# Two scan units of 64 groups in the S5 mixer, outputs multiplied from the states themselves, and another order of its steps

## The chip, the core and the metric

The kernel runs on one core of a Trainium2 chip. The metric is the device time of one execution in microseconds (us); less is better.

## The reference, cut to what matters

Two blocks in a row on 256 tokens of 1024 features. The first has a latent-attention layer and then an S5 layer, and a second block follows (two attentions and a gated feed-forward layer). The change lies in the S5 layer alone. It runs a diagonal complex state-space scan in two directions over 256 context tokens and then 256 latent tokens, for 128 groups of 16 channels with 64 complex states each:

```python
def step(h, u_chunk):
    bu = jnp.einsum('btgs,gps->btgp', u_chunk.astype(jnp.complex64), b_bar)
    a = jnp.broadcast_to(lam_bar, bu.shape)
    _, xs = lax.associative_scan(_ssm_combine, (a, bu), axis=1)
    xs = xs + powers[None] * h[:, None]
    y = jnp.einsum('btgp,gsp->btgs', xs, cmat).real
    return xs[:, -1], y
...
y = jax.nn.gelu(y.astype(g.dtype))
ya, yb = jnp.split(y @ w_glu + b_glu, 2, axis=-1)
return ((ya * jax.nn.sigmoid(yb)) * jax.nn.silu(g)) @ w_out
```

Here u and g are the two halves of `h @ w_in`, and y sums both directions and a skip term. Only the latent tokens are carried on.

## The kernel before, in words

Everything is float32; large products split an operand in a high and a low part and take three matmuls. Instructions are written in program order and a planner arranges them on each engine by its own costs, with the written order as priority, so that engines run in order but not always in the order of the text.

Tokens are held in chunks of 4, so that a direction has 64 chunks for the context and 64 for the latent tokens. The 128 partitions hold the 64 states of the forward direction (0 to 63) and of the backward one (64 to 127). The 128 groups are 16 tiles `m` of 8 groups. For each tile:

- `inputs(m)` multiplies `w_u` with the tokens, writes u to HBM (`ud`), and `take_back` reads it back in another layout (`U`).
- `chunk_sums(m)` multiplies U with the prepared input matrices `BT` (32 small matmuls), and ScalarE copies the results out: the context's sums to `Sc` (L1214), the latent ones to the unit's state array `Sl` (L1218). For every second tile a tree of VectorE operations (`scan_tree`, L1394) reduces the context to one state, which is put into `Cs` (L1226).
- `scan(un)` runs 63 sequential steps over the chunks of `Sl`, three VectorE operations each (`scan_step`, L1405: one multiplication to `ss`, two additions in place). `S5_UNITS` gives each of four units one block of 32 groups. `scan(...)` is a generator; `S5_PLAN` says how many steps of which units are written at which place, and two units named together are taken in turns.
- `direct(m)` starts the PSUM accumulation of the output with the part inside a chunk.
- `outputs(m)` (L1253) copies the states of the tile into `H` in chunk order, forward and backward (L1267 and L1268, ScalarE, the latter on VectorE for the tiles of `S5_DVE`), and multiplies `H` with `CC`: 16 matmuls with 128 rows. After each second tile ScalarE copies the sum to `Yb` (L1278), which goes to HBM (`yd`).
- `gate(m)` is the gate half of the projection with a Silu (L1285); `activate(b)` reads four tiles' y back, applies Gelu (L1294) and splits it; `glu(m)` begins the first six GLU tiles with the first half of y, and `s5_glu` (L1414) does the rest.

At the start of the kernel `s5_factors` (L920) makes the powers of the state matrix in `Lp` and the input factors in `Q` on VectorE; ScalarE copies them into the tables `FE` (L992 to L996).

Of the kernel before, what the change touches and what calls it, by code (L numbers as in the profile page):

```python
# [11 lines left out]
F32 = mybir.dt.float32  # L12
# [7 lines left out]
P = 128  # L20
# [62 lines left out]
S5_SPLIT = range(2, 8)  # L83
GLU_PLAIN = 3
GLU_EARLY = 6
S5_DVE = range(14, 16)
S5_UNITS = ((0,), (1,), (2,), (3,))

S5_PLAN = [("sums",0),("sums",1,(0,38)),("sums",2,(0,25),(1,25)),("sums",3,(1,25),(2,25)),("direct",0,4),("gates",0,5),("outputs",0,4),("scan",(1,13),(3,13)),("direct",4,8),("gates",5,13),("outputs",4,8),("direct",8,12),("scan",(2,38),(3,38)),("y",0,2),("gates",13,16),("outputs",8,12),("direct",12,16),("scan",(3,12)),("y",2,3),("glu",0,2),("outputs",12,16),("y",3,4),("glu",2,6)]

# [117 lines left out]
class Builder:  # L208
# [711 lines left out]
    def s5_factors(self, keep, pre):  # L920
# [37 lines left out]

        Lp = self.t(pre, [P, 2, P, 4]).rearrange("p r g s -> p r s g")
        ts(s2, cm, 1.0, None, ALU.add, ALU.bypass)  # L960
# [9 lines left out]

        Q = self.t(pre, [P, 2, P, 4]).rearrange("p r g s -> p r s g")
        self.tt(t1, re, re, ALU.mult)
# [166 lines left out]
    def s5(self):  # L1139
# [10 lines left out]
        ydw = self.yd.rearrange("(q j) o t c -> (j o t) q c", j=2)  # L1150
        U, Sl, Sc, Cs = {}, {}, {}, {}
        hh = []
# [35 lines left out]
        def chunk_sums(m):  # L1188
# [4 lines left out]
            if m == m0:  # L1193
                Sl[un] = [(late.pop(0) if late else self.s16([P, 4096])).rearrange("p (n r w) -> p n r w", r=2, w=w)
                          for _ in S5_UNITS[un]]
                Cs[un] = self.t(l1, [P, 2, w])
            if not od:
# [5 lines left out]
            for q in range(0, 4, 2):  # L1203
# [7 lines left out]
                for j in range(2):  # L1211
                    g0 = 2 * q + j
                    c0 = 8 * od + g0
                    nc.scalar.copy(S[:, :, :, c0:c0 + 3:2], ev(pS[j][:, :, :, 1]))  # L1214
                    c0 = 8 * (m - m0) + g0
                    for x, D in enumerate(Sl[un]):
                        n = D.shape[1]
                        nc.scalar.copy(D[:, :, :, c0:c0 + 3:2], ev(pS[j][:, :, :, 0, n * x:n * x + n]))  # L1218
            if not od:
# [3 lines left out]
            for l in range(6):  # L1223
                w, n = 1 << l, 32 >> l
                yield from self.scan_tree(S[:, w - 1::2 * w], S[:, 2 * w - 1::2 * w], LA[:, 4 * l:4 * l + 4], n)
            nc.vector.tensor_copy(Cs[un][:, :, 8 * (m - m0) - 8:8 * (m - m0) + 8], S[:, 63])  # L1226

        def scan(un):

            prev = Cs[un]  # L1230
            g0, w = 32 * S5_UNITS[un][0], 32 * len(S5_UNITS[un])
            n = 2048 // w
            for k in range(63):
                cur = Sl[un][k // n][:, k % n]
# [18 lines left out]
        def outputs(m):  # L1253
            un = unit[m // 4]
            C, S, m0 = Cs[un], Sl[un], 4 * S5_UNITS[un][0]
            CC = self.t(self.wp, [P, 8, 2, 64], F32, "wlo", 3)
            nc.sync.dma_start(out=CC.rearrange("p a b c -> p (a b c)"), in_=self.CCd[m])
            H = self.t(self.wp, [P, 2, 8, 64], F32, "whi", 3)
            g = slice(8 * (m - m0), 8 * (m - m0) + 8)
            hv = lambda x: x.rearrange("p c r g -> p r g c")  # L1260
            nc.scalar.copy(H[f, :, :, 0], C[f, :, g])
            nc.scalar.copy(H[b, :, :, 63], C[b, :, g])
            copy = nc.vector.tensor_copy if m in S5_DVE else nc.scalar.copy
            for x, D in enumerate(S):
                n = D.shape[1]
                k = min(n, 63 - n * x)
                nc.scalar.copy(H[f, :, :, 1 + n * x:1 + n * x + k], hv(D[f, :k, :, g]))  # L1267
                copy(H[b, :, :, 63 - n * x - k:63 - n * x], hv(D[b, k - 1::-1, :, g]))  # L1268
            py = pys.pop(m)
            for q in range(4):  # L1270
                for j in range(2):
                    for ri in range(2):
                        self.mm(py[64 * j:64 * j + 64, m % 2, q], CC[:, 2 * q + j, ri], H[:, ri, 2 * q + j], False,
                                m % 2 == 1 and q == 3 and ri == 1)
            done[m] = self.last
            if m % 2:
                Y = self.t(l1, [P, 8, 64], F32, "Yb", 2)
                nc.scalar.copy(Y, py.rearrange("p m q c -> p (m q) c"))  # L1278
                nc.scalar.dma_start(out=ydw[:, 4 * m - 4:4 * m + 4], in_=Y)

        def gate(m):
            ps = self.ps("b", (P, NL))
            self.linear32(ps, "w_u", 16 + m, self.h1, lat)
            sg = self.t(l1, [P, NL], F32, "sg", 2)
            nc.scalar.activation(sg, ps, AF.Silu)  # L1285
            nc.scalar.dma_start(out=self.sgd[m], in_=sg)

        def activate(b):
# [4 lines left out]
            nc.gpsimd.dma_start(out=y, in_=self.yd[32 * b:32 * b + 32].rearrange("(i g) o t c -> (g o) i (t c)", i=4))  # L1293
            nc.scalar.activation(y, y, AF.Gelu_apprx_tanh)  # L1294
            with self.tc.issue_after(self.step_last):
# [3 lines left out]
        def glu(m, k0=0, k1=KT, after=None):  # L1299

            if k0 == 0:
                self.pp.append(self.ps("a" if m < 4 else "b", (P, 2, NL)))
            pp = self.pp[m]
# [564 lines left out]
```

## Time and profile before

| what | us |
|---|---|
| median of 3 runs | 1421.99 |
| lowest, highest | 1419.64, 1423.6 |
| the profiled execution's own time | 1420.1 |
| its span, first to last instruction | 1418.3 |
| TensorE (PE) busy | 1343.9 (95%) |
| PE weight loads | 1146.2 (81%) |
| VectorE (DVE) busy | 1053.4 (74%) |
| ScalarE (ACT) busy | 826.2 (58%) |

The page is of one execution. Busy shares are averages over stages of different kinds; the S5 stage lies between about 500 and 810 us of the span.

### The profile page before, as it was taken

The page shows a single profiled execution, that of the slowest core. Times are in us where ns is not written, and L with a number is a line of the kernel's source. Part 1 is how long each engine was busy: PE and PEld are TensorE (multiplying, and loading weights), DVE is VectorE, ACT ScalarE, POOL GpSimd, SP SyncE. Part 2 cuts the span into 40 slices and gives each one's busy share as a digit, 9 for nine tenths or more (in the row PEclk, how much of TensorE's full clock was granted, in tenths as well). Part 3 has the DMA queues.
Part 4 walks back from the last instruction along what each step waited for, and adds up shares of the span by engine and source line. Part 5 has one row for each costly group of instructions (what it writes and reads, how often), then busy time and mean ns, then how long its engine had stood idle before and what let it go on. Part 6 is the DMA issues. An engine that isn't in the chain of part 4 may idle for free.

```text
span 1418.3 us, 26373 instructions
## 1 busy us (share of the span) xinstructions
PE 1343.9 (95%) x10042; PEld 1146.2 (81%) x10042; DVE 1053.4 (74%) x2546; ACT 826.2 (58%) x1433; POOL 95.7 (7%) x150
## 2 busy tenths in 40 slices
PE   5899999999999999788988999999999999999999
PEld 1577777887788667346877899999979999999999
DVE  6779768988789959899994465556667777788853
ACT  4598755665556854337367654444468664666642
POOL 1012100000012223220000000000000000000000
PEclk9999999999999999999999999999999999999999
DMA  8546633134275459665865766655434435555564
GB/s 307 203 172 225 200 116 127 56 116 139 85 269 188 145 163 317 211 195 145 249 211 190 247 206 197 191 188 186 155 110 133 143 130 164 173 185 180 185 185 136
DMA packets 105487, 252.60 MB, mean 178 GB/s; under 512 B 37168, under 2 KB 45744, under 8 KB 104976
## 3 DMA queue, kind: packets, MB, share of 16 engines
q1 hardware_dynamic: 77056, 204.50, 44.5%
q0 software_dynamic: 7344, 25.04, 5.4%
q10 hardware_dynamic: 20960, 21.37, 4.6%
q8 instruction: 79, 1.29, 0.4%
q14 instruction: 48, 0.39, 0.1%
HBM read 218.88 MB, written 34.08 MB: 178 GB/s over the span
## 4 chain that ended last, share of the span: by engine, by line
PE 70%; ACT 11%; DVE 8%; DMA 7%; issue 3%; ACTq 1%; POOL 0%; SPq 0%; POOLq 0%; DVEq 0%
PE a L228 57%; PE b L228 9%; DVE bt L284 2%; PE c L228 1%; ACT whi L240 1%; DMA ud<-Ub 1%; ACT whi L1267 1%; ACT zc L1102 1%; DVE wlo L284 1%; ACT whi L1268 1%; DMA raw<-in_w_glu 1%; ACT zc L1099 1%; DMA Ul<-Td 1%; PE c L671 1%; DVE s L284 1%
## 5 line engine op out<-in xcount | busy, mean ns | idle before, releaser
L228 PE MATMUL a<-s,whi 128*128 128x256 f32 (+2 forms) x3024 | 644.8, 310 | 2.1 <-ACT whi L240 2.1
L228 PEld LDWEIGHTS a<-s,whi 128*128 128x128 f32 x3024 | 494.0, 191 | 33.2 <-issue 4.3
L228 PE MATMUL a<-s,wlo 128*128 128x256 f32 (+1 forms) x1512 | 464.2, 309 | 0.6 <-DVE wlo L284 0.6
L284 DVE TENSOR_TENSOR wlo<-raw,whi 128x1024 fp32r<-128x1024 f32 (+2 forms) x234 | 280.8, 1201 | 193.7 <-ACT whi L240 192.7
L240 ACT CAST whi<-raw 128x1024 fp32r<-128x1024 f32 (+2 forms) x234 | 240.8, 1031 | 244.1 <-PE a L228 178.1
L228 PEld LDWEIGHTS a<-s,wlo 128*128 128x128 f32 x1512 | 289.3, 192 | 15.2 <-DVE wlo L284 1.2
L228 PE MATMUL a<-s,raw 128*128 128x512 f32 (+2 forms) x272 | 109.9, 556 | 17.7 <-DVE s L483 6.6
L228 PEld LDWEIGHTS a<-s,raw 128*128 128x128 f32 x272 | 53.8, 202 | 63.0 <-issue 38.6
L284 DVE TENSOR_TENSOR bt<-x,bc 128x512 f32<-128x512 f32 x128 | 83.4, 691 | 8.3 <-DMA bc<-in_bc 7.1
L284 DVE TENSOR_TENSOR s<-s,ss 128x64 f32<-128x64 f32 x504 | 87.6, 219 | 2.6
L228 PE MATMUL a<-x,whi 128*128 128x256 f32 (+1 forms) x384 | 74.2, 294 | 0.0
L284 DVE TENSOR_TENSOR ss<-x,s 128x128 f32<-128x128 f32 x248 | 62.5, 284 | 1.2
L228 PE MATMUL b<-s,raw 128*128 128x256 f32 x256 | 58.9, 387 | 3.1 <-ACT sg L1285 3.1
L228 PEld LDWEIGHTS a<-x,whi 128*128 128x128 f32 x384 | 60.4, 192 | 0.6
L228 PEld LDWEIGHTS b<-s,raw 128*128 128x128 f32 x256 | 48.4, 193 | 10.3 <-ACT sg L1285 3.7
L228 PE MATMUL a<-x,wlo 128*128 128x256 f32 (+1 forms) x192 | 56.1, 292 | 0.0
L284 DVE TENSOR_TENSOR sc<-LA,Sc 128x1024 f32<-128x1024 f32 (+5 forms) x96 | 44.2, 500 | 12.7 <-ACT Sc L1214 12.4
L228 PEld LDWEIGHTS a<-U,whi 64*64 64x64 f32 x1024 | 31.9, 140 | 21.3 <-ACT Ub L1178 10.7
L284 DVE TENSOR_TENSOR Sc<-Sc,sc 128x1024 f32<-128x1024 f32 (+5 forms) x96 | 48.0, 500 | 0.4
L228 PE MATMUL a<-U,whi 64*64 64x128 f32 x1024 | 37.5, 286 | 11.3 <-ACT Ub L1178 7.5
L733 DVE TENSOR_REDUCE st<-b 128x1 f32<-128x512 f32 (+1 forms) x64 | 34.8, 550 | 16.6 <-PE b L228 16.1
L240 ACT CAST s<-s 128x512 fp32r<-128x512 f32 (+1 forms) x48 | 25.9, 545 | 21.9 <-DVE s L284 14.8
(384 smaller groups left out, 2249.8 us busy)
## 6 DMA issues: line engine op xcount, KB each, us to landing
raw<-in_w_glu SPq DMA_DIRECT2D x64, 512.0 KB, 3.6
raw<-in_w_up SPq DMA_DIRECT2D x42, 512.0 KB, 3.5
raw<-in_w_out SPq DMA_DIRECT2D x40, 512.0 KB, 3.7
raw<-in_wmod SPq DMA_DIRECT2D x32, 512.0 KB, 3.6
raw<-in_w_u SPq DMA_DIRECT2D x32, 512.0 KB, 3.9
s<-in_wmod SPq DMA_DIRECT2D x16, 512.0 KB, 7.7
raw<-in_w_in SPq DMA_DIRECT2D x16, 512.0 KB, 4.3
BTd<-BT ACTq DMA_DIRECT2D x16, 512.0 KB, 3.5
```

Of the source, the lines that this page charges most:

```text
L228: self.last = self.ins(self.nc.tensor.matmul(out, l, r, start=start, stop=stop))
L240: self.nc.scalar.copy(hi, src)
L284: return self.ins(self.nc.vector.tensor_tensor(out, a, b, op=op))
L671: nc.tensor.transpose(pt[:, k, tt], pl[tt][:, (2 * b + k) * P:(2 * b + k + 1) * P], self.ident)
L733: nc.vector.tensor_reduce(st[:, 0:1], ps, axis=AX.X, op=ALU.max)
L1099: nc.scalar.copy(zt[b, :, 0:3], ct[b, :, 1:4])
L1102: nc.scalar.copy(zt[f, :, 4:7], ct[f, :, 0:3])
L1267: nc.scalar.copy(H[f, :, :, 1 + n * x:1 + n * x + k], hv(D[f, :k, :, g]))
L1268: copy(H[b, :, :, 63 - n * x - k:63 - n * x], hv(D[b, k - 1::-1, :, g]))
```

## The change

It gives each of two units two blocks (64 groups), so there are 126 steps of twice the width and no longer 252. The context's final state goes to slot 0 of `Sl`, the sums of chunk i to slot i + 1, so that the states stand where the outputs need them; `Cs` and `H` and their copies are gone, and `outputs` multiplies straight from `Sl`: for each group, part and state tile one matmul for the forward half (64 rows, into `py`) and one for the backward half read in reverse (64 rows, into a second PSUM tile `pb`), 32 columns each. `py` and `pb` are added on VectorE. Gelu is ordered behind the last gate's Silu. `Lp` and `Q` are laid out with the groups innermost. The GLU tiles 2 and 3 take PSUM tag "b", all others "a". `S5_PLAN` is another: sums 0 and 1 without scans, unit 0 scanned in sums 2 and 3 with five gates between them, unit 1 scanned alone in three parts after the sums.

```diff
-S5_DVE = range(14, 16)
-S5_UNITS = ((0,), (1,), (2,), (3,))
-S5_PLAN = [("sums",0),("sums",1,(0,38)),("sums",2,(0,25),(1,25)),("sums",3,(1,25),(2,25)),("direct",0,4),("gates",0,5),("outputs",0,4),("scan",(1,13),(3,13)),("direct",4,8),("gates",5,13),("outputs",4,8),("direct",8,12),("scan",(2,38),(3,38)),("y",0,2),("gates",13,16),("outputs",8,12),("direct",12,16),("scan",(3,12)),("y",2,3),("glu",0,2),("outputs",12,16),("y",3,4),("glu",2,6)]
+GLU_B = (2, 3)
+S5_UNITS = ((0, 1), (2, 3))
+S5_PLAN = [("sums",0),("sums",1),("sums",2,(0,30)),("gates",0,5),("sums",3,(0,33)),("direct",0,4),("gates",5,10),("outputs",0,4),("scan",(1,20)),("direct",4,8),("gates",10,14),("outputs",4,8),("scan",(1,20)),("direct",8,12),("gates",14,16),("y",0,2),("scan",(1,23)),("direct",12,16),("glu",0,2),("outputs",8,12),("y",2,3),("glu",2,4),("outputs",12,16),("y",3,4),("glu",4,6)]
...
-        Lp = self.t(pre, [P, 2, P, 4]).rearrange("p r g s -> p r s g")
+        Lp = self.t(pre, [P, 2, 4, P])
...
-        Q = self.t(pre, [P, 2, P, 4]).rearrange("p r g s -> p r s g")
+        Q = self.t(pre, [P, 2, 4, P])
...
                     for x, D in enumerate(Sl[un]):
                         n = D.shape[1]
-                        nc.scalar.copy(D[:, :, :, c0:c0 + 3:2], ev(pS[j][:, :, :, 0, n * x:n * x + n]))
+                        k = int(x == 0)
+                        nc.scalar.copy(D[:, k:, :, c0:c0 + 3:2], ev(pS[j][:, :, :, 0, n * x + k - 1:n * x + n - 1]))
...
-            H = self.t(self.wp, [P, 2, 8, 64], F32, "whi", 3)
...
-            for x, D in enumerate(S):
-                n = D.shape[1]
-                k = min(n, 63 - n * x)
-                nc.scalar.copy(H[f, :, :, 1 + n * x:1 + n * x + k], hv(D[f, :k, :, g]))
-                copy(H[b, :, :, 63 - n * x - k:63 - n * x], hv(D[b, k - 1::-1, :, g]))
-            py = pys.pop(m)
+            if m % 2 == 0:
+                pys["b"] = self.ps("a", (P, 2, 4, 64))
+            py, pb = pys.pop(m), pys["b"]
             for q in range(4):
-                for j in range(2):
-                    for ri in range(2):
-                        self.mm(py[64 * j:64 * j + 64, m % 2, q], CC[:, 2 * q + j, ri], H[:, ri, 2 * q + j], False,
-                                m % 2 == 1 and q == 3 and ri == 1)
+                for ri in range(2):
+                    for j in range(2):
+                        g = 2 * q + j
+                        for x, D in enumerate(S):
+                            n = D.shape[1]
+                            o = slice(64 * j, 64 * j + 64), m % 2, q
+                            end = m % 2 == 1 and q == 3 and ri == 1 and x == len(S) - 1
+                            v = D[:, :, ri, 8 * (m - m0) + g]
+                            self.mm(py[o][:, n * x:n * x + n], CC[f, g, ri], v[f], False, end)
+                            self.mm(pb[o][:, 64 - n * x - n:64 - n * x], CC[b, g, ri], v[b, ::-1],
+                                    m % 2 == 0 and q == 0 and ri == 0 and x == 0, end)
             done[m] = self.last
             if m % 2:
                 Y = self.t(l1, [P, 8, 64], F32, "Yb", 2)
-                nc.scalar.copy(Y, py.rearrange("p m q c -> p (m q) c"))
+                nc.scalar.copy(Y, pb.rearrange("p m q c -> p (m q) c"))
+                self.tt(Y, py.rearrange("p m q c -> p (m q) c"), Y, ALU.add)
...
-            nc.scalar.activation(sg, ps, AF.Silu)
+            self.gate_last = self.ins(nc.scalar.activation(sg, ps, AF.Silu))
...
-            nc.scalar.activation(y, y, AF.Gelu_apprx_tanh)
+            with self.tc.issue_after(self.gate_last):
+                nc.scalar.activation(y, y, AF.Gelu_apprx_tanh)
...
-                self.pp.append(self.ps("a" if m < 4 else "b", (P, 2, NL)))
+                self.pp.append(self.ps("b" if m in GLU_B else "a", (P, 2, NL)))
```

## Rows read from the trace of the kernel before

**Rows 1.** The page: its span, and the chain that ended last, by engine.

```profile
span 1418.3 us, 26373 instructions
...
PE 70%; ACT 11%; DVE 8%; DMA 7%; issue 3%; ACTq 1%; POOL 0%; SPq 0%; POOLq 0%; DVEq 0%
```

**Rows 2.** Windows: length, then busy of PE, PEld, DVE, ACT, POOL; clock; DMA.

```profile
560.00:600.00 40.00, 32.44 (x248) 16.35 (x247) 33.33 (x114) 13.99 (x37) 8.44 (x13) 0.91 0.73 231
700.00:800.00 100.00, 85.21 (x763) 75.39 (x762) 67.17 (x349) 71.76 (x80) 3.01 (x4) 0.97 0.69 214
560.00:800.00 240.00, 206.83 (x1830) 154.32 (x1829) 199.08 (x910) 133.77 (x218) 24.20 (x33) 0.95 0.67 206
```

**Rows 3.** Waits of PE, 560 to 800 us: total us, times, longest.

```profile
PE c L228 <- ACT whi L1268: 4.8, 3, 2.8
```

**Rows 4.** Timeline of DVE: the trees' copies to Cs of tiles 7 and 15, last scan step.

```profile
600.48 0.17 DVE L1226 COPY x<-Sc 128x32 f32<-128x32 f32 x1
...
685.73 0.17 DVE L1226 COPY x<-Sc 128x32 f32<-128x32 f32 x1
...
762.35 0.49 DVE L284 TENSOR_TENSOR s<-s,ss 128x64 f32<-128x64 f32 x2
```

**Rows 5.** Timeline of PE: runs of small matmuls, and one GLU tile's first half.

```profile
102.83 0.97 PE L228 MATMUL c<-zc,zb 128*32 128x112 f32 x32
...
565.95 1.98 PE L228 MATMUL a<-U,whi 64*64 64x128 f32 x64
...
684.56 2.55 PE L228 MATMUL c<-whi,wlo 128*64 128x64 f32 x78
...
749.65 7.17 PE L228 MATMUL a<-hl,raw 128*128 128x256 f32 x32 [2.72 <-DMA raw<-in_w_glu]
```

**Rows 6.** Groups by form, whole span: count, then busy us, mean ns, idle before.

```profile
L240 ACT CAST whi<-raw 128x1024 fp32r<-128x1024 f32 x220 | 230.4, 1049 | 230.4 <-PE a L228 168.6 <-issue 43.3 <-DMA raw<-in_w_up 4.2
...
L284 DVE TENSOR_TENSOR s<-s,ss 128x64 f32<-128x64 f32 x504 | 87.6, 219 | 2.6
...
L284 DVE TENSOR_TENSOR ss<-x,s 128x128 f32<-128x128 f32 x248 | 62.5, 284 | 1.2
...
L1267 ACT COPY whi<-s 64x1008 f32<-64x1008 f32 x16 | 31.4, 1960 | 2.1 <-DVE s L284 1.9
...
L1218 ACT COPY s<-a 128x256 f32<-128x256 f32 x64 | 27.2, 425 | 0.0
...
L228 PE MATMUL c<-whi,wlo 128*64 128x64 f32 x512 | 20.4, 233 | 4.8 <-ACT whi L1268 4.8
...
L284 DVE TENSOR_TENSOR sc<-LA,Sc 128x256 f32<-128x256 f32 x16 | 6.0, 417 | 0.1
...
L284 DVE TENSOR_TENSOR Sc<-Sc,sc 128x128 f32<-128x128 f32 x16 | 4.5, 282 | 0.1
```

**Rows 7.** Timeline of DVE: two neighbouring steps of interleaved scans, and of one alone.

```profile
744.29 0.49 DVE L284 TENSOR_TENSOR ss<-x,s 128x128 f32<-128x128 f32 x2
...
745.24 0.49 DVE L284 TENSOR_TENSOR ss<-x,s 128x128 f32<-128x128 f32 x2
...
760.33 0.29 DVE L284 TENSOR_TENSOR ss<-x,s 128x128 f32<-128x128 f32 x1
...
761.18 0.29 DVE L284 TENSOR_TENSOR ss<-x,s 128x128 f32<-128x128 f32 x1
```

**Rows 8.** Timeline of DVE and PE at the start: strided, unstrided, first large matmuls.

```profile
16.41 2.06 DVE L284 TENSOR_TENSOR cm<-x 128x512 f32<-128x512 f32 x2
...
28.38 2.49 DVE L284 TENSOR_TENSOR s<-s,s 128x512 fp32r<-128x512 f32 x4
...
26.58 6.26 PE L228 MATMUL a<-s,raw 128*128 128x512 f32 x8 [6.58 <-DVE s L483]
```

**Rows 9.** Timeline of ACT and PE: last copy of y, first of the second halves.

```profile
790.89 0.59 ACT L1278 COPY Yb<-c 128x512 f32<-128x512 f32 x1 [1.32 <-PE c L228]
...
808.86 0.40 PE L228 MATMUL a<-s,whi 128*128 128x256 f32 x2
```

More of the change, by code (lines that the diff above doesn't have):

```diff
@@ L1150, in s5 @@
         ydw = self.yd.rearrange("(q j) o t c -> (j o t) q c", j=2)
-        U, Sl, Sc, Cs = {}, {}, {}, {}
+        U, Sl, Sc = {}, {}, {}
         hh = []
@@ L1195, in chunk_sums @@
                           for _ in S5_UNITS[un]]
-                Cs[un] = self.t(l1, [P, 2, w])
             if not od:
@@ L1225, in chunk_sums @@
                 yield from self.scan_tree(S[:, w - 1::2 * w], S[:, 2 * w - 1::2 * w], LA[:, 4 * l:4 * l + 4], n)
-            nc.vector.tensor_copy(Cs[un][:, :, 8 * (m - m0) - 8:8 * (m - m0) + 8], S[:, 63])
+            nc.vector.tensor_copy(Sl[un][0][:, 0, :, 8 * (m - m0) - 8:8 * (m - m0) + 8], S[:, 63])
         def scan(un):
-            prev = Cs[un]
+            prev = Sl[un][0][:, 0]
             g0, w = 32 * S5_UNITS[un][0], 32 * len(S5_UNITS[un])
             n = 2048 // w
-            for k in range(63):
+            for k in range(1, 64):
                 cur = Sl[un][k // n][:, k % n]
@@ L1254, in outputs @@
             un = unit[m // 4]
-            C, S, m0 = Cs[un], Sl[un], 4 * S5_UNITS[un][0]
+            S, m0 = Sl[un], 4 * S5_UNITS[un][0]
             CC = self.t(self.wp, [P, 8, 2, 64], F32, "wlo", 3)
             nc.sync.dma_start(out=CC.rearrange("p a b c -> p (a b c)"), in_=self.CCd[m])
-            H = self.t(self.wp, [P, 2, 8, 64], F32, "whi", 3)
[L1259 to L1263, printed above, removed]
-            for x, D in enumerate(S):
-                n = D.shape[1]
-                k = min(n, 63 - n * x)
-                nc.scalar.copy(H[f, :, :, 1 + n * x:1 + n * x + k], hv(D[f, :k, :, g]))
-                copy(H[b, :, :, 63 - n * x - k:63 - n * x], hv(D[b, k - 1::-1, :, g]))
-            py = pys.pop(m)
-            for q in range(4):
-                for j in range(2):
-                    for ri in range(2):
-                        self.mm(py[64 * j:64 * j + 64, m % 2, q], CC[:, 2 * q + j, ri], H[:, ri, 2 * q + j], False,
-                                m % 2 == 1 and q == 3 and ri == 1)
+            if m % 2 == 0:
+                pys["b"] = self.ps("a", (P, 2, 4, 64))
+            py, pb = pys.pop(m), pys["b"]
+            for q in range(4):
+                for ri in range(2):
[9 more added lines that the diff above has]
+                                    m % 2 == 0 and q == 0 and ri == 0 and x == 0, end)
             done[m] = self.last
```

## The prediction, made before the changed kernel was run

> **What bounds the kernel now.** I read the page first: PE holds 70% of the chain that ended last, ACT 11%, DVE 8% [rows 1]. So time is won where PE idles and lost where PE gets more to do. The windows over the S5 stage show where it idles: from 560 to 800 us it is busy 206.8 of 240, which leaves 33.2 us, of them 7.6 before 600 (sums of tiles 4 to 7) and 14.8 after 700 [rows 2]; so 10.8 lie in 600 to 700. The waits say for what: one of the longer ones is the copies of the states, but it is only 4.8 us [rows 3]. The other engine to watch is DVE. Its last tree before 600 ends at 600.5, the last of all at 685.7, and the last scan step at 762.4 [rows 4]. From 600 to 700 it is the sums and scans that fill it; behind 762 PE works off what waited for the last states, and the first second half of the GLU begins at 808.9 [rows 9]. From there on the kernel is unchanged, so I ask by how much this 808.9 moves.
>
> **The change part by part.**
>
> *Outputs.* The copies go: 16 forward ones of 1.96 us, 31.4 us on ACT, and nearly as much for the backward ones [rows 6]. But ACT is not the bound; all PE ever waited for them is 4.8 us [rows 3], inside the 33.2. In return PE's work grows. Before, a tile has 16 matmuls; all 16 tiles together are 256, which the trace shows as 512 records, two for each float32 matmul, with 20.4 us busy [rows 6]. Now a tile has 4 x 2 x 2 groups and parts, two state tiles and two directions: 64 matmuls, 128 records; over 16 tiles 2048. Their price is the main unknown, since no row has 64 rows by 64 with 32 columns. The near ones are 0.97/32 = 30 ns (32 wide, 112 columns), 1.98/64 = 31 ns (64 by 64, 128 columns) and 2.55/78 = 33 ns (64 wide, 64 columns) [rows 5]. The columns differ by two and the price hardly, so I take 30.5 ns: 62.5 us, that is +42. The bounds: if the price fell with the columns, 31 x 32/128 = 8 ns, 16 us in all, -4. If the stream set the pace, see next, it is 62 ns and 127 us, +107.
>
> The states are read with a step of 128 floats, where H was unbroken. What a step costs is seen on other engines: ACT copies the stepped states at 1960/1008 = 1.94 ns per column and an unbroken tile at 1049/1024 = 1.02 [rows 6]; DVE takes 1.03 us for 512 strided columns against 0.62 for unbroken ones [rows 8]. On PE no row shows it. Thirty-two columns at 1.94 ns are 62 ns, the upper bound. I keep 30.5 because forward and backward halves sit on different partitions, so that two streams at 62 would still give 31 per record.
> The Trainium skill ("SBUF — State Buffer", section "Door 1: The DMA port swizzle") says that SBUF has 16-byte lines and that each access to a new line pays; the ACT and DVE rows just named agree, and by it the upper bound would be the sum. It also ("TensorE: Matmul & The Clock Gate", section "Wait — 56ns, not 53.3ns?") gives matmuls a floor of about 25 ns from start to start however few columns; the three runs of 30 to 33 ns agree with such a floor, and at 25 ns the outputs would be an estimated 51 us, +31.
>
> *Scans.* A step alone takes 0.85 us, two interleaved ones 0.945, so 0.47 each [rows 7]. Twice the width makes the multiplication 417 instead of 284 ns and each addition 282 instead of 219 [rows 6]: +0.26 us, so 1.11 alone and 0.73 when something else fills the gaps. The trees of tiles 8 to 15 and all that was scanned with them took 600.5 to 685.7 [rows 4]. A pair of tiles' tree is 24 operations over 8064 columns; from 417 and 282 ns for 256 and 128 columns [rows 6] a column costs 1.05 ns and an operation 0.15 us besides, 12 us in all, four of them 48; unit 0's 63 steps between them are 46 more, so the trees end at some 694, 8 later. I add nothing for the two neighbouring steps of one unit that now wait for each other, though it could be 10. Then unit 1 scans alone, 63 x 1.11 = 70 us, and four additions of Y of 0.7 us stand between: 767 against 762.4. Half the operations, and no gain: the two interleaved scans had filled the gaps that the single one leaves open.
>
> *Copies of the sums.* Each copy of L1218 becomes two, of 31 and 32 chunks, four more ACT instructions per tile. 64 copies at 425 ns become 128 of about 300 (the fixed part is what is left of 425 without half the columns): +11 us on ACT. From 600 on DVE paces the sums and covers it; before 600 the sums go round PE and ACT, six tiles, up to 0.6 us each: I take +1, bounds 0 and 4.
>
> *Order, Gelu, PSUM tags.* Five gates go between sums 2 and 3, into idle time of PE; if it weren't there they would cost what they did after the sums. Gelu behind the last Silu spares table loads of ACT: nothing on the path, up to 3 us if one stood before the last y. What waits behind that Gelu on ACT are the splits of y, and glu waits for those; the gates end well before unit 1 does, which covers it. The tags change who holds which bank: "a" now carries both pb and four GLU tiles; nothing, or a wait of a few us at the end.
>
> *Start.* `Lp` and `Q` unstrided: a product of 512 columns costs 0.62 instead of 1.03 us [rows 8]. The three `cmul` calls and single writes stream some 4,900 strided columns; at (1.03 - 0.62)/512 = 0.8 ns that is 4 us on DVE, and PE waits 6.6 us just there for DVE [rows 8]. Against it the eight table copies of ACT become stepped reads, 512 x 0.92 = 0.5 us more each; they have slack behind the casts. I take -3.5, bounds -4 and +1.
>
> **The sum.** By PE's work: +42, less the idle that the new order can fill. The 7.6 before 600 is out of its reach; of the 25.6 after it I let 18 be filled, since the last y must still go out and come back. 42 - 18 + 1 - 3.5 = +21. By the chain behind the scan: 767, then eight tiles of outputs, 8 x 3.9 = 31, then 18 from the last output to the first second half as now (790.9 to 808.9) [rows 9], 816: +7, and with -3.5 + 1 about +5; every GLU tile that the plan puts between the outputs adds up to 7.2 [rows 5]. The two are bounds of one event; PE's work is the later one, but the planner may fill more than I allow (all 25.6: +14). I take +16. The profiled execution took 1420.1 us (span 1418.3): 1436. The median stands 1.9 higher: **1438**.
>
> **The rivals.**
> *The small matmuls overlap (0.19).* If four quarters of the array run side by side at about 16 ns per record, the outputs cost 33 us, +13, and 13 - 18 + 1 - 3.5 = -8: 1414, faster. The place is `outputs`; the sign turns where 2048 r = 20.4 + 18 + 2.5 us, at 20 ns. For it: 64-by-64 matmuls of 128 columns already run at 31 ns. Against it: runs of quite different widths and columns are all at 30 to 33.
> *The chain behind the scan decides (0.16).* Stalls of single steps, Y additions that wait for PE in front of scan steps, and two GLU tiles (some 13 us) between the outputs: 10 + 5 + 13 on top of +5 gives +33, 1455. For it: in both orders the last outputs stand behind the last step on DVE [rows 4]; against it: PE has other work to do meanwhile.
> *Stepped reads pace PE (0.08).* Quarters on the same partitions share their stream, 62 ns: +107 - 22, about 1505. For it the ACT and DVE rows; against it, that PE reads two halves at once.
> *It cancels (0.07).* At 20 to 24 ns or with all idle filled: 1418 to 1426.
>
> **How the numbers follow.** The main case, PE's extra work at 28 to 33 ns, has 0.50 and a range of its own of 1426 to 1450. To 8 in 10 I reach down to 1412, into half of the overlap rival, and up to 1465, past the scan rival; that leaves out half of 0.19 and the 0.08. A change of 0.3%, 4.3 us, is about what a measurement of this kernel can tell from none. Faster: the overlap rival and a little of the cancelling one, 0.20; within: 0.08; slower: 0.72.
>
> **What would show it.** PE: 2048 output records, at 28 to 33 ns in unbroken runs; a run of a whole tile in 3.6 to 4.2 us. DVE: 1.1 us per step of unit 1 alone, its end at 764 to 775. ACT's busy time in the stage some 50 us less, with no gain. PE's idle in the stage below 20 us and the first second half of the GLU at 820 to 830 (less what the start gains). At the start PE's large matmuls begin 3 to 4 us sooner. I am wrong if a tile's outputs take under 2.5 us or above 6, or if the idle of PE doesn't shrink.

## The result, and the profile after

The changed kernel takes 1468.3 us (median of 4 runs, 1463.3 to 1469.8) against 1422.8 beside it: a ratio of 1.0307, 95% interval 1.0263 to 1.0352. It is slower by 45.5 us; the forecast was 16, and the time lies outside its range. The profiled execution took 1463.3 us. First the page of the changed kernel: its span and its chain by engine, to be read beside [rows 1].

```profile
span 1461.5 us, 29060 instructions
...
PE 65%; DVE 19%; ACT 7%; DMA 5%; issue 3%; ACTq 0%; POOL 0%; SPq 0%; DVEq 0%; POOLq 0%
```

VectorE's share has gone from 8% to 19%. The windows, with the columns of [rows 2]; the last four lines are the whole stage from the first split inputs to the first Sigmoid, the scan after the trees, all up to the first second half, and one tile of outputs.

```profile
560.00:600.00 40.00, 32.50 (x293) 16.80 (x295) 24.12 (x65) 16.08 (x51) 11.01 (x16) 0.91 0.71 206
700.00:800.00 100.00, 78.20 (x1527) 69.96 (x1525) 64.74 (x189) 11.32 (x21) 1.51 (x2) 0.80 0.49 145
560.00:800.00 240.00, 203.94 (x2516) 155.30 (x2514) 185.28 (x537) 57.16 (x178) 22.39 (x31) 0.88 0.57 171
...
504.00:863.00 359.00, 315.49 (x4047) 252.13 (x4048) 239.48 (x625) 97.92 (x286) 40.55 (x51) 0.90 0.61 187
...
693.00:766.45 73.45, 54.99 (x1143) 49.97 (x1142) 67.06 (x201) 3.94 (x8) 0.75 (x1) 0.74 0.49 143
766.45:852.45 86.00, 77.25 (x1327) 71.57 (x1326) 15.93 (x25) 19.16 (x30) 2.25 (x3) 0.90 0.58 172
...
709.50:712.25 2.75, 2.57 (x128) 2.41 (x128) 2.51 (x8) 0.00 (x0) 0.00 (x0) 1.00 0.23 88
```

ScalarE has 77 us less to do from 560 to 800, and nothing comes of it. TensorE does less there than before, at a granted clock of 0.88 in place of 0.95; from 693 to 766, while unit 1 is scanned alone, the clock is 0.74, so about half of the stretch is at the 1.2 GHz level. The same stage of the kernel before is 308 us with TensorE busy 273.0:

```profile
509.00:817.00 308.00, 273.00 (x2499) 210.46 (x2500) 242.78 (x996) 164.61 (x287) 40.65 (x51) 0.96 0.70 217
```

It is 51 us longer now, 42.5 of it busy and 8.5 idle. Where these 51 us lie is seen from four moments in the timelines of VectorE, TensorE and ScalarE.

```profile
592.85 0.18 DVE L1227 COPY s<-Sc 128x32 f32<-128x32 f32 x1
...
692.87 0.17 DVE L1227 COPY s<-Sc 128x32 f32<-128x32 f32 x1
...
714.90 0.68 DVE L284 TENSOR_TENSOR Yb<-c,Yb 128x512 f32<-128x512 f32 x1
...
733.19 0.68 DVE L284 TENSOR_TENSOR Yb<-c,Yb 128x512 f32<-128x512 f32 x1
...
765.89 0.62 DVE L284 TENSOR_TENSOR s<-s,ss 128x128 f32<-128x128 f32 x2
766.42 0.68 DVE L284 TENSOR_TENSOR Yb<-c,Yb 128x512 f32<-128x512 f32 x1
```

```profile
22.88 5.40 PE L228 MATMUL a<-s,raw 128*128 128x512 f32 x8 [2.72 <-DVE s L483]
...
733.92 3.68 PE L228 MATMUL c<-Ul,x 128*128 128x64 f32 x16 [8.34 <-DVE Yb L284]
...
774.74 5.25 PE L228 MATMUL a<-hl,raw 128*128 128x256 f32 x16 [0.63 <-ACT hl L1295]
```

```profile
716.04 0.59 ACT L1277 COPY Yb<-a 128x512 f32<-128x512 f32 x1 [8.02 <-DVE ss L284]
...
771.91 0.39 ACT L1285 ACTIVATE sg<-b 128x256 f32<-128x256 f32 x1 [3.91 <-PE b L228]
...
773.62 1.07 ACT L1295 ACTIVATE hl<-hl 128x1024 f32<-128x1024 f32 x1
778.08 1.06 ACT L1295 ACTIVATE hl<-hl 128x1024 f32<-128x1024 f32 x1 [3.40 <-DMA hl<-yd]
...
839.74 0.59 ACT L1277 COPY Yb<-a 128x512 f32<-128x512 f32 x1 [8.95 <-PE a L228]
```

The trees end at 693.0 (before 685.9), the last step at 766.5 (before 762.8) [rows 4], the last outputs at 839.7 (before 790.9), and the second halves begin at 852.4, when the 96 records of the last two first halves are through (before 808.9 [rows 9]). So the trees end 7 us later (12 later if counted from the stage's start, which is 5 us sooner), the scan gains 3, and the tail from the last step to the second halves grows from 46 to 86. Most of the loss is in the tail. Added up from its timeline, TensorE has in it 26 us of outputs, 29 of GLU tiles 0 to 3, 7 of `direct`, 3 of the last gates and 9 of waits up to the last copy of Y, and then 13 of GLU tiles 4 and 5. Before, the first half of a GLU tile stood at 749.7 [rows 5], beside the scan; now the first begins at 774.7. The y of tiles 4 to 7 is back only at 778.1, as the addition of its last two tiles comes on VectorE at 766.4, behind the last scan step. The y of tiles 0 to 3 is back at 743.8 (fetched by GpSimd at 738.7, below, 5.1 us to landing), but its Gelu runs at 773.6: the change orders Gelu behind the last Silu, and that one comes at 771.9.

```profile
738.68 0.75 POOL L1293 DMA_DIRECT2D hl<-yd  x1 [74.70 <-DMA yd<-Yb]
```

TensorE's longest waits from 560 to 860:

```profile
PE c L228 <- DVE Yb L284: 13.2, 3, 8.3
PE a L228 <- issue: 6.3, 5, 2.1
PE c L228 <- issue: 6.0, 3, 3.9
```

`Yb` is the addition on VectorE that the change brings: the second one begins at 733.2, 17 us after ScalarE's copy at 716.0, with 16 scan steps ahead of it, and only then does `direct` get its PSUM bank. `issue`, a wait for nothing that the profile shows, comes mostly between tiles of outputs. Of the groups by form, as [rows 6], the outputs into `c` (those into `a` run beside them) and the two copies that took the place of one:

```profile
L228 PE MATMUL c<-s,wlo 64*64 64x32 f32 x1024 | 47.8, 268 | 3.2 <-issue 2.1 <-DMA wlo<-CCd 1.0
...
L1219 ACT COPY s<-a 128x128 f32<-128x128 f32 x64 | 21.6, 337 | 0.0
...
L1219 ACT COPY s<-a 128x124 f32<-128x124 f32 x64 | 20.4, 319 | 0.0
```

Counting each moment of TensorE for the record that began last, the outputs take 50.6 us (19.7 before), and the gates, `direct` and first halves of the GLU, the same matmuls as before, 125.0 (113.7 before). So of the 42.5 us more of busy time 31 are outputs, and 11 are equal work at a lower clock; and as 12.3 of the idle time are pauses inside the outputs, all other idle is 3.8 us less than before.

### The profile page after: what moved, and what is told of

It is laid out like the page before. It is cut to its first block, busy times and chain, and to the rows that moved or that the text cites. A ratio compares the mean times of both kernels' runs of the same rounds, so it can differ in the third digit from the quotient of the medians.

```text
span 1461.5 us, 29060 instructions
## 1 busy us (share of the span) xinstructions
PE 1382.7 (95%) x11578; PEld 1184.8 (81%) x11578; DVE 1046.2 (72%) x2174; ACT 762.9 (52%) x1431; POOL 95.0 (7%) x150
## 4 chain that ended last, share of the span: by engine, by line
PE 65%; DVE 19%; ACT 7%; DMA 5%; issue 3%; ACTq 0%; POOL 0%; SPq 0%; DVEq 0%; POOLq 0%
PE a L228 54%; PE b L228 7%; DVE s L284 5%; DVE ss L284 3%; PE c L228 2%; DVE Sc L284 2%; DVE sc L284 2%; DVE bt L284 2%; DVE wlo L284 2%; ACT whi L240 1%; ACT zc L1102 1%; DMA whi<-BTd 1%; PE c L671 1%; ACT zc L1099 1%; DMA To<-Ysb 1%
## 5 line engine op out<-in xcount | busy, mean ns | idle before, releaser
L228 PEld LDWEIGHTS a<-s,whi 128*128 128x128 f32 x3056 | 499.2, 192 | 31.7 <-issue 4.8
L228 PE MATMUL a<-s,wlo 128*128 128x256 f32 (+2 forms) x2552 | 516.3, 293 | 7.0 <-issue 6.3
L228 PEld LDWEIGHTS a<-s,wlo 128*128 128x128 f32 (+1 forms) x2552 | 337.6, 183 | 19.7 <-issue 5.0
L284 DVE TENSOR_TENSOR s<-s,ss 128x128 f32<-128x128 f32 x252 | 73.7, 294 | 6.8
L228 PE MATMUL b<-s,raw 128*128 128x256 f32 x256 | 63.7, 408 | 3.1 <-DMA raw<-in_w_u 2.5
L228 PEld LDWEIGHTS b<-s,raw 128*128 128x128 f32 x256 | 51.7, 206 | 11.5 <-DMA raw<-in_w_u 1.9
L284 DVE TENSOR_TENSOR ss<-x,s 128x256 f32<-128x256 f32 x126 | 53.3, 424 | 3.3
L228 PEld LDWEIGHTS c<-s,wlo 64*64 64x64 f32 x1024 | 45.2, 169 | 9.4 <-issue 7.5
L228 PE MATMUL c<-s,wlo 64*64 64x32 f32 x1024 | 47.8, 268 | 3.2 <-issue 2.1
```

The costliest lines, as they stand in the source:

```text
L228: self.last = self.ins(self.nc.tensor.matmul(out, l, r, start=start, stop=stop))
L284: return self.ins(self.nc.vector.tensor_tensor(out, a, b, op=op))
```

## The experiments

Three theories, by the numbers that the expectations use. **The queue theory** (1): what was ready stands in an in-order queue behind what is not, and TensorE's work slides behind the scan; at first I took the additions of Y on VectorE for what blocks. **The scan theory** (2): unit 1 alone sets the end. **The work theory** (3), that of the forecast: the outputs are more work for TensorE. Ratios are to the kernel before, run beside each.

### Parts of the change by themselves

`start_only`: the kernel before with the two layouts.

```diff
-        Lp = self.t(pre, [P, 2, P, 4]).rearrange("p r g s -> p r s g")
+        Lp = self.t(pre, [P, 2, 4, P])
```

> The kernel before with only the layout of Lp and Q changed. The start's term alone: 4 to 5 us less, 1417 to 1419, as the first matmuls of the S5 inputs begin 4.8 us sooner in the changed kernel (508.9 to 504.1). If the sooner start is eaten by later waits: 1421 to 1423.

1419.1 against 1421.8, 0.998 (0.9969 to 0.9991): 2.8 us, nearly all of the start's term.

`gelu_tags`: the kernel before with the order of Gelu and the PSUM tags.

```diff
+            with self.tc.issue_after(self.gate_last):
+                nc.scalar.activation(y, y, AF.Gelu_apprx_tanh)
...
+                self.pp.append(self.ps("b" if m in GLU_B else "a", (P, 2, NL)))
```

> The kernel before with two small edits alone: Gelu ordered behind the last Silu written, and PSUM tag b for the GLU tiles 2 and 3 (a for the others). If these are harmless, as forecast: 1420 to 1425. If they are what makes all kernels with direct outputs 20 us slower: 1435 to 1445.

1419.7 against 1421.2, 0.9992 (0.9974 to 1.001): harmless. `start_tags` is the kernel before with both edits:

```diff
+        Lp = self.t(pre, [P, 2, 4, P])
...
+            with self.tc.issue_after(self.gate_last):
```

> The kernel before with only the harmless small parts of the change: the layout of Lp and Q (0.998 alone), Gelu behind the last Silu written, and the PSUM tags of the GLU tiles (0.999 alone). If the parts add, 1416 to 1419; if the start's gain is lost in later waits, 1420 to 1422.

1413.4 against 1423.0, 0.9936 (0.9919 to 0.9952). This is the version that beats both kernels; why it wins more than its two parts is not known.

`units_plan`: the kernel before with the changed units and order, but with `H`, its copies and 16 matmuls per tile.

```diff
-S5_UNITS = ((0,), (1,), (2,), (3,))
+S5_UNITS = ((0, 1), (2, 3))
+S5_PLAN = [("sums",0),("sums",1),("sums",2,(0,30)),("gates",0,5),("sums",3,(0,33)),("direct",0,4),("gates",5,10),
...
```

> The kernel before, with two units of 64 groups and the changed order of steps, but still with the copies into H, 16 matmuls per tile and no addition of Y. Theory 1: no addition of Y and no larger outputs, so only the scan's 5 us and what the other order costs: 1420 to 1435. Theory 2 (unit 1 alone sets the end): 1450 to 1465. Theory 3 (outputs are the loss): 1418 to 1428.

1445.7 against 1421.8, 1.0177 (1.016 to 1.0194). Half of the whole loss is there without one direct output. VectorE waits 8.6 us in front of the splits of y, which stand ahead of the last scan steps; the scan ends at 779.4. `y_late` moves them behind:

```diff
-("y",0,2),("scan",(1,23)),
+("scan",(1,23)),("y",0,2),
```

> The kernel with wide units, copies and the changed order (1445.7), but the first two parts of y written behind the last part of the scan. There VectorE stands 8.6 us in front of the splits of y, among the steps of unit 1, and the scan ends at 778.8. If that wait is on the path, the scan ends near 768 and the time is 1434 to 1440. If the work that is left behind the scan sets the end, the GLU tiles that are now later take back what is won: 1443 to 1448.

1443.9 against 1423.9, 1.0143 (1.012 to 1.0167): the scan ends at 771.4 and the time hardly moves; the second forecast held. `order_only` has the new order with four narrow units:

```diff
+("sums",1),("sums",2,(0,30),(1,30)),("gates",0,5),("sums",3,(0,33),(1,33)),
...
+("scan",(2,20),(3,20)),
```

> The kernel before with its four units of 32 groups and its copies, but with the changed kernel's order of steps; where that names a wide unit, the two narrow ones are taken in turns. Against the kernel with wide units and the same order (1445.7): if the order is the loss (half of all outputs behind the last scan step, y's splits between scan steps), 1440 to 1450; if the width is (63 steps of 1.11 us alone, 70 us, against 63 pairs at 0.945, 60 us), 1422 to 1432.

1445.6 against 1423.9, 1.0146 (1.0128 to 1.0165), against 1.0177 for the same order with wide units: the width of a step has at most some 4 us. So the scan theory falls: it is mainly the order, not the width of a step; but wide units force part of that order, as unit 0 can't be scanned before sums 1 is done. Here too VectorE stands in front of y, among scan steps (its timeline):

```profile
756.57 0.43 DVE L284 TENSOR_TENSOR s<-hl,s 128x256 fp32r<-128x256 f32 x1 [13.82 <-ACT s L240]
```

`gates_moved`: of the new order only the five early gates.

```diff
-("sums",3,(1,25),(2,25)),("direct",0,4),("gates",0,5),
+("gates",0,5),("sums",3,(1,25),(2,25)),("direct",0,4),
```

> The kernel before with one thing of the new order: the first five gates between sums 2 and 3, and not behind direct 0 to 4; units, scans (from sums 1 on) and all else stay. Against the kernel with narrow units and the whole new order (1445.6): if the gates spent early are what is missing later as work for TensorE beside the scan, 1432 to 1445; if it is the scans' start, which the new order moves from sums 1 to sums 2, 1420 to 1427.

1428.0 against 1421.2, 1.0046 (1.002 to 1.0072): some 7 us (3 to 10), between both forecasts' cases. That the gates are missed as work beside the scan is not shown: in this run's trace TensorE is as busy from 685.9 to 763.2 as before (65.5 and 65.7 us), and the last outputs end at 790.9 as before.

### Where Y is added

`sum_pool`: the changed kernel with the addition off VectorE.

```diff
-                self.tt(Y, py.rearrange("p m q c -> p (m q) c"), Y, ALU.add)
+                Z = self.t(l1, [P, 8, 64], F32, "Ub", 2)
+                nc.scalar.copy(Z, py.rearrange("p m q c -> p (m q) c"))
+                nc.gpsimd.tensor_tensor(Y, Y, Z, op=ALU.add)
```

> The changed kernel, with the addition of Y taken off VectorE: ScalarE copies both sums out of PSUM and GpSimd adds them. Theory 1 (additions of Y stand behind scan steps on VectorE, so that the PSUM banks of tag c and ScalarE's queue are released late): the three waits of PE for Yb (13.2 us) go, and part of the stretches at the lower clock behind them; 1440 to 1452. Theory 2 (unit 1, scanned alone, sets the end whatever PE does): 1464 to 1470, the waits of PE only change their name. Theory 3 (the outputs themselves are the loss): below 1 us of difference from the changed kernel's 1468 in the outputs, and a gain of no more than the 13 us.

1466.3 against 1421.8, 1.032 (1.0301 to 1.034): nothing won, and my first form of the queue theory, that the addition is the cause, falls. The wait has only moved. TensorE and ScalarE in this run:

```profile
758.14 0.31 PE L228 MATMUL c<-s,wlo 64*64 64x32 f32 x2
771.90 3.42 PE L228 MATMUL c<-s,wlo 64*64 64x32 f32 x60 [13.45 <-DVE s L284]
775.24 5.05 PE L228 MATMUL a<-hl,raw 128*128 128x256 f32 x16
```

```profile
759.95 2.00 ACT L1297 ACTIVATE hl<-hl 128x1024 f32<-128x1024 f32 x2
```

The Gelu of y 0 to 7 is done at 762, so the first GLU tile could run; it stands at 775 behind outputs of tile 8 that wait 13.5 us for the last scan step.

### The order of TensorE's queue

`glu_first`: as `sum_pool`, with TensorE kept in the written order from the first GLU tile on.

```diff
-("direct",12,16),("glu",0,2),
+("direct",12,16),("order",),("glu",0,2),
```

> The changed kernel with the addition of Y on GpSimd (1466.3), and on TensorE the first two GLU tiles kept ahead of the outputs of tiles 8 to 15, as they are written. There TensorE stands 13.5 us in front of the first outputs of tile 8, until the last scan step is done, while the y of tiles 0 to 7 is back and through Gelu at 762. If the order of TensorE's queue is what wastes the end of the scan, GLU tiles go into the wait: 1450 to 1458. If the time is set by the outputs and GLU tiles that are left when the scan ends, whatever their order: 1463 to 1468.

1447.8 against 1421.2, 1.0192 (1.0147 to 1.0237): 18.5 us less than `sum_pool`, by order alone. Now a GLU tile lies beside the scan's end, and the second one ahead of the outputs:

```profile
758.56 9.29 PE L228 MATMUL a<-hl,raw 128*128 128x256 f32 x34 [2.84 <-ACT hl L1297]
770.56 6.74 PE L228 MATMUL a<-hl,raw 128*128 128x256 f32 x30 [2.71 <-DMA raw<-in_w_glu]
```

`tail_order` goes further, all outputs ahead of GLU tiles 2 to 5.

```diff
-("y",2,3),("glu",2,4),("outputs",12,16),("y",3,4),("glu",4,6)]
+("y",2,3),("outputs",12,16),("y",3,4),("glu",2,6)]
```

> The changed kernel with the addition on GpSimd and the first two GLU tiles first (1447.8), and then all outputs of tiles 8 to 15 ahead of GLU tiles 2 to 5. There the last outputs end at 823.9 and 23.6 us of GLU work stand before the first Sigmoid. If the tail is bound by TensorE's work, nothing is won by order: 1444 to 1449. If the return of the last y sets the end, the last outputs end 13 us sooner and most of it is won: 1434 to 1440.

1463.8 against 1423.0, 1.0281 (1.026 to 1.0303): worse than either forecast. The last outputs do end sooner, at 812, but ScalarE copies the last Y only at 820.5, behind a cast of GLU weights, and the casts for the next GLU tiles stand behind the Gelu of the last y:

```profile
820.50 0.59 ACT L1277 COPY Yb<-a 128x512 f32<-128x512 f32 x1
822.56 0.37 ACTq L1281 DMA_DIRECT2D yd<-Yb  x1
835.74 1.06 ACT L1297 ACTIVATE hl<-hl 128x1024 f32<-128x1024 f32 x1 [14.65 <-DMA hl<-yd]
```

```profile
839.15 0.80 PE L228 MATMUL a<-s,whi 128*128 128x256 f32 x2 [11.05 <-ACT whi L240]
```

### The outputs' matmuls

`direct_only`: the changed kernel with the units and the order of before. A state tile then holds 64 chunks, and a tile of outputs takes 64 records of 64 columns.

```diff
-S5_UNITS = ((0, 1), (2, 3))
+S5_UNITS = ((0,), (1,), (2,), (3,))
```

> The changed kernel with the units and the order of steps of before: four units of 32 groups, so that a state tile holds all 64 chunks and an output tile takes 32 matmuls of 64 columns (64 records) instead of 64 of 32. If the outputs are paced by the number of instructions (3.3 to 3.9 us per tile of 128 records in the changed kernel), a tile takes 1.7 to 2.0 us: 30 us in all, 10 more than before; less the start's 4.8, and with waits for additions of Y behind shorter steps: 1424 to 1435. If they are paced by the stepped reads (62 ns per 32 columns), a tile takes 7 us and the time is above 1480. If units and order are the whole loss: 1418 to 1422.

1443.4 against 1421.8, 1.0161 (1.0141 to 1.018): 8 us above the forecast. `direct_unbroken` has the same instructions reading neighbouring floats:

```diff
-                            v = D[:, :, ri, 8 * (m - m0) + g]
+                            v = D[:, n - 1].rearrange("p r w -> p (r w)")
```

> The same as the kernel with direct outputs and the units and order of before (1443), but each matmul of the outputs reads 64 neighbouring floats of the last chunk's states instead of 64 floats at a step of 64; so the output is computed from other data, and the instructions, their waits and their order stay. There a tile's 64 records take 2.2 to 2.4 us, four of them starting together every 0.137 us, which is 2.1 ns per column; the matmuls with U, whose columns lie side by side, come to 0.97 ns. If the step is what paces them: a tile takes about 1.0 to 1.3 us, the outputs 16 to 20 instead of 37 us, and the time is 1422 to 1430. If small matmuls cost some 30 ns each whatever they read: 1437 to 1443.

1444.3 against 1423.9, 1.014 (1.012 to 1.0159). One tile in each run, stepped first (windows):

```profile
735.90:738.45 2.55, 2.53 (x65) 2.30 (x66) 2.55 (x18) 0.00 (x0) 0.00 (x0) 1.00 0.85 227
```

```profile
735.28:736.48 1.20, 1.18 (x65) 1.11 (x65) 1.20 (x9) 0.00 (x0) 0.00 (x0) 1.00 1.01 396
```

The step doubles the price of a tile, as that theory had it; all 16 take 36.6 us with it and 20.1 without (counted as above), about what they take in the kernel before. And the time stays, against the forecast. Over the whole stage, again stepped first (windows):

```profile
480.60:838.10 357.50, 319.57 (x3114) 243.38 (x3113) 263.65 (x1034) 119.06 (x262) 48.89 (x61) 0.93 0.65 196
```

```profile
480.30:839.60 359.30, 309.96 (x3113) 233.78 (x3112) 263.71 (x1034) 118.51 (x260) 48.95 (x61) 0.91 0.64 194
```

What the outputs give up, waits and the clock take: TensorE's idle rises from 37.9 to 49.3 us, and gates, `direct` and plain GLU tiles take 10 us more. `after_unbroken` does the same to the changed kernel:

```diff
+                            v = D[:, n - 1, ri, 0:n]
```

> The changed kernel, but each matmul of the outputs reads 32 neighbouring floats of a state tile's last chunk instead of 32 floats at a step of 128; so the output is computed from other data, all else stays. If the step alone paces the outputs: a tile goes from 2.5 us and a pause to about 1.0 us, and the time falls by 20 or more, to 1440 to 1450. If the instruction stream paces them (in the changed kernel a packet of 16 KB of PE's instructions is fetched every 3.5 to 4.3 us while outputs run, and PE pauses 1.2 to 2 us after each tile): a tile with its pause stays at 3.3 to 3.9 us, the pauses grow as the matmuls shrink, and the time stays at 1460 to 1468.

1466.7 against 1423.9, 1.0307 (1.028 to 1.0333), as the instruction theory had it: the outputs take 46.3 us in place of 50.6, the waits for `issue` 17.3 in place of 12.3, together 63.6 and 62.9. One tile, to be read beside the 2.57 us above:

```profile
709.13:711.20 2.07, 2.07 (x128) 1.96 (x128) 1.89 (x6) 0.00 (x0) 0.00 (x0) 1.00 0.34 131
```

Its waits for `issue` from 560 to 860:

```profile
PE a L228 <- issue: 10.6, 5, 3.6
PE c L228 <- issue: 6.7, 3, 4.5
```

In the old order, then, less work of the outputs wins nothing by itself, and there the work theory falls. In the changed kernel the outputs with their pauses cost TensorE as much unbroken as stepped, so this pair can't tell what less work would win.

### Direct outputs in the old order

`direct_only` has the first GLU tile behind the outputs of tiles 8 to 11, as the changed kernel has. Four more runs, all with Y added on GpSimd: `unbroken_pool` changes no order.

> Direct outputs with the units and the order of before, reading neighbouring floats (so the output is computed from other data; 1444.3), with the addition of Y moved to GpSimd behind two copies of ScalarE. TensorE's outputs take no longer there than in the kernel before (20.1 against 19.5 us), and still it is 21 us slower. If the addition of Y behind scan steps is why (it holds back y, Gelu, and behind them ScalarE's queue), 1424 to 1434; if the small matmuls themselves (the clock, the fetches of instructions) are, 1440 to 1446.

1439.6 against 1421.2, 1.0132 (1.0093 to 1.0171): at most 5 us from the addition. `direct_first` and, with neighbouring floats, `unbroken_first`:

```diff
-("outputs",8,12),("direct",12,16),("scan",(3,12)),("y",2,3),("glu",0,2),("outputs",12,16),
+("order",),("glu",0,2),("outputs",8,12),("direct",12,16),("scan",(3,12)),("y",2,3),("outputs",12,16),
```

> Direct outputs with the units and scans of before (1443.4), the addition of Y on GpSimd, and the first two GLU tiles ahead of the outputs of tiles 8 to 15 in TensorE's queue, the other four behind all outputs. There TensorE's queue has all 128 matmuls of tiles 8 to 11 ahead of the first GLU tile, which the kernel before has not. If that order is what costs 20 us, what is left is the outputs' work (36.7 against 19.5 us) less the start: 1426 to 1436. If direct outputs cost 20 us by other means: 1438 to 1443.

> The same, with the matmuls of the outputs reading 64 neighbouring floats (so the output is computed from other data). Their work is then that of the kernel before, 20 us. If queue order and work are all, 1414 to 1426; if something else of the direct outputs costs 20 us, 1434 to 1440.

1453.5 and 1450.3 against 1423.0, 1.0222 (1.0199 to 1.0245) and 1.0189 (1.0164 to 1.0213): slower than both forecasts, with the same 11 us wait behind ScalarE's last Gelu as in `tail_order`. `direct_tail` and `unbroken_tail` put GLU tiles 2 and 3 ahead of the last outputs:

```diff
-("y",2,3),("outputs",12,16),("y",3,4),("glu",2,6)]
+("y",2,3),("glu",2,4),("outputs",12,16),("y",3,4),("glu",4,6)]
```

> As the run with GLU tiles 0 and 1 first in the old units (1453.5), but with GLU tiles 2 and 3 ahead of the outputs of tiles 12 to 15 again, so that their casts on ScalarE stand ahead of the last Gelu. The 11 us wait of TensorE for these casts should go: 1438 to 1445. If the outputs' own work (17 us more than before, less the start's 3) is all that is left, 1432 to 1438; if something else holds it, 1445 or more.

> The same with outputs that read 64 neighbouring floats (so the output is computed from other data) and take as long as before. If work and queue order are all there is, 1418 to 1428; if small matmuls cost more than their time (the lower clock, the fetches of instructions, waits elsewhere), within 5 us of the run beside it.

1448.4 and 1445.6 against 1422.2, 1.0175 (1.0129 to 1.0221) and 1.015 (1.0107 to 1.0192). The 11 us wait is gone, and still neither is near the kernel before. TensorE's waits from 660 to 845, `direct_tail` and then `unbroken_tail`:

```profile
PE c L228 <- DMA x<-To: 7.8, 1, 7.8
PE c L228 <- DVE s L284: 5.0, 1, 5.0
...
PE c L228 <- DMA wlo<-CCd: 2.0, 2, 1.6
```

```profile
PE c L228 <- DMA wlo<-CCd: 13.3, 5, 4.5
PE c L228 <- DMA x<-To: 6.0, 1, 6.0
```

With quicker matmuls the tables `CC` come too late (13.3 us for 2.0), and what the work gives up the wait takes. That these loads are the rest of the 20 us that direct outputs cost in the old order was not tried; it stays open.

## Why the prediction was wrong, point by point

- **The idle of TensorE, the step that failed.** By the sum, "of the 25.6 after it I let 18 be filled", and the +16 that I took fills 23. From 560 to 800 the idle is 36.1 us, and was 33.2 [rows 2]; over the stage it grew by 8.5. In it are the 12.3 us of pauses that the forecast's 62.5 for the outputs already holds, so the other idle fell by 3.8, not by 18 to 23. These 14 to 19 us, and the 11 of the clock, for which the sum had no term, make about the 27 us between the 1436 forecast for the profiled execution and its 1463.3. The forecast took idle time for a store that any work can draw on. Shown: TensorE's queue head waits for the last step while work behind it is ready (13.5 us in `sum_pool`), and the written order, with GLU tiles 0 and 1 ahead of the outputs of tiles 8 to 15, wins 18.5 us.
- **The chain behind the scan** was the other bound of the same event. Its 767 for the last step is right (766.5); its 18 for the way back of y came to 12.7. What failed in it is "eight tiles of outputs, 8 x 3.9 = 31": 73 us lie between the last step and the last outputs. The outputs themselves take 26 of them; 29 are GLU tiles 0 to 3, and the rest is `direct`, gates and waits. The rival (0.16, 1455) had this mechanism with two GLU tiles; there were four.
- **The outputs.** 62.5 us were forecast, and 50.6 busy with 12.3 of pauses were measured, 62.9: the sum is right by luck, since neither part was forecast. A tile takes 2.57 us and so 20 ns per record, not 30.5: the rival in which four quarters overlap was right in its premise. The pauses nobody had. What the step costs on TensorE depends on the record: a tile of 32-column records takes 2.57 us with it and 2.07 without, one of 64-column records 2.53 and 1.18. Of the rules of the Trainium skill named there, that of the 16-byte lines ("SBUF — State Buffer", section "Door 1: The DMA port swizzle") agrees with 2.53 us stepped for 1.18 unbroken; the floor of about 25 ns from start to start ("TensorE: Matmul & The Clock Gate", section "Wait — 56ns, not 53.3ns?") doesn't, at 20 and 18 ns per record with four quarters at work. That the work's size decides by itself is refuted for the old order of scans by three pairs of stepped and unbroken reads, each pair with one plan, which agree within some 3 us (1443 and 1444, 1454 and 1450, 1448 and 1446): waits and the clock took what the work gave up. For the changed kernel (1468 and 1467) it stays open, as its pauses grew by what the matmuls gave up.
- **The scans** ended as forecast: last step 766.5 for 767, trees' end 693.0 for 694, "Half the operations, and no gain". The trees' end is luck in part: the last four trees with the scan between them took 100.0 us, not 94, and began at 593.0 in place of 600.6.
- **Copies of the sums**: 42.0 us for 27.2 on ScalarE, +14.8 for +11, covered. **Start**: 26.6 [rows 8] to 22.9 in the profile, 2.8 us in the median, for 3.5.
- **Gelu and tags**: nothing in the old order. But "the gates end well before unit 1 does" was wrong: the last Silu comes at 771.9, the last step ends at 766.5. And it is not only the splits of y that wait there: GLU tiles 0 to 2 multiply the y that Gelu writes. The Gelu of the first four tiles ran 30 us after their y was back. What that costs no run shows, as none takes this order out of the changed kernel.
- **The gates** "into idle time of PE": costed at nothing, 6.8 us measured in the old order. By what way stays open.
- **The clock** had no term. It was 0.88 for 0.95 from 560 to 800; gates, `direct` and GLU tiles, the same matmuls as before, take 11 us more in the stage.

So 18.5 of the 45.5 us are shown with their cause, the order of TensorE's queue from the first GLU tile on (in runs that add Y on GpSimd). 27 are left (29 without the start's gain), and their cause stays open. The early gates cost 7 in the old order. The rest goes with the new order, in which scans and outputs start later, and with direct outputs; each of the two costs some 22 alone and both together no more than 27 once the queue is right, so they hide behind each other, and no run parts them.

## What to carry to other kernels

Idle time is only worth filling if the head of the queue can run: before counting it, name the work that is ready at that moment, and check that nothing unready stands ahead of it on its engine. Work that is free to move (here the gates) is not free of cost when it is spent early: ask what it leaves behind. An order put between two instructions (here Gelu behind the last Silu) can be harmless in one order of the steps and hold data back for 30 us in another. A change that makes half of a stage wait for one event puts the whole backlog behind that event: sum what then stands there, with all that is ordered between.

## What the runs showed of the hardware

- **Instruction supply.** While outputs run, from 701 to 715, the instruction queue q8, which I take for TensorE's, brings four packets of 16 KB, and one in the GLU from 860 to 874 (the DMA view):

```profile
q8 instruction: 4, 0.07, 2.1%
```

  The windows have 508 matmuls and 506 weight loads in the first of these stretches, 119 and 118 in the second: some 250 instructions for each packet both times, so a tile of 128 records uses up one. TensorE stood still eight times for `issue`, 0.5 to 3.9 us each time, and in seven of them it went on 1.3 to 1.6 us after such a packet had landed. With matmuls made shorter the sum of work and pauses stayed (62.9 and 63.6 us). So a stream of tiny matmuls has a pace of its own, some 3.9 us per 128 records here. It doesn't hold from the first record on: in `glu_first`, right behind a GLU tile, some 250 records run without a pause (windows):

```profile
777.25:782.15 4.90, 4.90 (x252) 4.79 (x251) 0.00 (x0) 0.35 (x1) 0.00 (x0) 1.00 0.81 281
```

  That the packets set the pace was not tried by itself.
- **Quarters of the array and stepped reads.** 64 records of 64 by 64 with 64 columns take 1.18 us unbroken, 18 ns each, and 2.53 us at a step of 64 floats; 128 with 32 columns take 2.07 us unbroken, 16 ns each, and 2.57 at a step of 128 floats. The Trainium skill ("TensorEngine Tiling (Array Packing)", section "Tiling Modes") has four independent tiles of 64 by 64. The trace agrees: in the stepped run four records start together every 0.14 us.
- **The clock** fell to the 1.2 GHz level not only behind long waits. From 701 to 715 the changed kernel's TensorE was busy with outputs for 10.95 of 14 us at full clock, with no pause over 1.5 us, and from 716.4 to 723.3, at `direct` and gates, the granted clock was 0.50 (windows):

```profile
701.00:715.00 14.00, 10.95 (x508) 10.01 (x506) 12.73 (x39) 0.62 (x1) 0.00 (x0) 1.00 0.43 156
716.42:723.25 6.83, 6.83 (x23) 5.84 (x23) 6.21 (x19) 0.20 (x1) 0.00 (x0) 0.50 0.87 200
```
